# Block products by Strassen's scheme in the projections of an attention and retention block

## The chip, the cores and the metric

The kernel runs on one core of a Trainium2 chip. The metric is the device time of one execution in microseconds (us). Engines are named as in the profile: PE is TensorE (PEld its weight loads), DVE is VectorE, ACT is ScalarE, POOL is GpSimd, SP is SyncE, whose queue issues all the transfers here.

## The reference

For x of 4096 tokens by 1024 features (float32, one layer):

```python
u = rms_norm(h, pre_norm_gain)
proj = einsum('bsd,de->bse', u, w_in)                # 1024 -> 4104
fq, fk, fv, fz, ff, rq, rk, rv, rz = split(proj)     # 4 x 512, 8, 4 x 512
fox = forgetting_attention(fq, fk, fv, ff + bias)    # 8 heads of 64, causal
fox = fox * silu(fz)
ret = retention(rq, rk, rv)                          # 4 heads of 128, rotary, chunks of 64, group norm
ret = ret * silu(rz)
out = einsum('bse,ed->bsd', concat(fox, ret), w_out) # 1024 -> 1024
h = h + rms_norm(out, post_norm_gain)
```

## The kernel before, in words

Float32 precision is had from float16 matmuls: each operand is split into a high and a low float16 part, and a product is three passes, high by high, high by low and low by high (`PASSES`, line 29; `unit`, line 367). A block is 512 tokens; there are 8. A projection unit is 128 output rows by 512 columns with the whole depth of 1024, that is 8 depth steps by 3 passes: 24 matmuls of 512 columns into one PSUM bank. "T" units put output features on the partitions (queries and keys), "N" units put tokens there (values and gates). The weights come in groups of 1024 columns: group 0 and group 1 are the attention heads 0 to 3 and 4 to 7, groups 2 and 3 the retention heads, group 4 is `w_out`.

The program has three stages.

- **Group 0** (`phase_f0`, line 539). For each block: x is loaded, normalised (`a_norm`), turned by PE, split (`a_k`) and stored in DRAM as `XT`; four T units, then four N units of two matmuls each, of 256 and 264 columns because the 8 forget logits ride along. DVE and ACT evacuate.
- **Attention with fills** (`attention`, line 1035). 1152 steps of 128 keys by 512 queries. A step has on PE two score matmuls, a matmul for the running maximum of a later item (`max_tile`, DVE reduces it from PSUM) and twelve of 64 or 65 columns that apply the weights to the values; on ACT two exponentials of 512 columns; on POOL a subtraction. Between steps a generator of fills emits projection work of groups 1, 2 and 3 (`fill_f1`, `fill_r`) and the retention, as much as a credit allows: `FILL_COST` and `ATT_COST` are PE times that set the ratio, `RMIN` its floor.
- **The output projection** (`fill_o`, line 1150). It needs all heads of a block, so most of it comes after the last attention step. For each of 32 tiles of 128 tokens: row maximum and scaling, 8 transposes, a split, 48 matmuls of 512 columns, and the second norm.

Every instruction order is the program's own (`tc.manual_schedule`). Evacuations are generators (`spawn`) that go one step further at each `tick`; so each engine's queue is in the order of the ticks, and an engine whose next instruction waits holds up all behind it. PSUM is a pool of eight banks, `PS` (line 93), shared by projection units, score tiles, maxima, the attention's sums and the retention. Weights are split by `w_split` (line 210) into pools of 16 tiles a half (`wt`, `wn`), so that two groups fit; their maxima, for scaling, are taken by `scales` (line 281).

```python
    def unit(outs, lhs, rhss):
        for k in range(KT):
            for i, (pw, px) in enumerate(PASSES):
                for o, r in zip(outs, rhss):
                    mm(o, lhs(k, pw, px), r(k, pw, px), k == 0 and i == 0, k == KT - 1 and i == 2)
            yield k
```

Of the kernel before, what the change touches and what calls it, by code (L numbers as in the profile page):

```python
# [16 lines left out]
D = 1024  # L17
KT = 8
# [10 lines left out]
PASSES = ((0, 0), (0, 1), (1, 0))  # L29
COST_MM = 216.0  # L30
WARM = 28
PUMP = (2, 6)
# [7 lines left out]
FILL_COST = 1.121e6  # L40
ATT_COST = 1.05e6
# [3 lines left out]
RMIN = 1.0  # L45
FRESH = 4
# [7 lines left out]
def kernel(  # L54
# [23 lines left out]
    KC = max(8, NB + 1)  # L78
    BUFS = dict(wt=16, wn=16, rw=2, xh=8, xt=4, kc=KC, vt=KC, s4=5, xq=4, lq=2, s2=8, z1=4, pf=2, ph=6, pl=6, sm=14, mk=2, qk=4, mr=2)
# [5 lines left out]
    SHARED = {t: "b2" for t in ('s2', 'pf', 'rw')}  # L85
# [64 lines left out]
    XT = DR("XT", [NB, KT, 128, 2, 512], F16)  # L150
# [42 lines left out]
    def w_raw(g, part, k, tag="rw"):  # L193

        rows = slice(k * 128, (k + 1) * 128)
        raw = SB(tag, [128, 512 + (FH if g == 0 and part else 0)])
        if g == 4:
            dma(raw, wo2[rows, part * 512 : (part + 1) * 512])
            return raw
        base = 0 if g < 2 else 2048 + FH  # L200
        src = w2[rows, base : base + 2048].rearrange("p (s c) -> p s c", s=4)[:, 2 * part : 2 * part + 2, (g % 2) * 256 : (g % 2) * 256 + 256]
        if g == 0 and part:
            dma(raw[:, 512:520], w2[rows, 2048 : 2048 + FH])
        dma(raw[:, 0:512].rearrange("p (s c) -> p s c", s=2), src)
        return raw
# [3 lines left out]

    def w_split(g, part, k, raw, W):  # L210

        tag = w_tag(g, part)
        n = raw.shape[1]
        wt = SB(tag, [128, 2, 512 + (FH if tag == "wn" else 0)], F16)
        hi, lo = wt[:, 0, 0:n], wt[:, 1, 0:n]
        gk = gsc[g][part][:, k : k + 1]
        nc.scalar.activation(out=hi, in_=raw, func=AF.Copy, scale=gk)
        yield 1
        stt(lo, raw, gk, hi, ALU.mult, ALU.subtract)
        for _ in range(WAGE):  # L220
            yield 1
        W.append(wt)

    def w_max(mk, i, raw):
        nc.vector.tensor_reduce(out=mk[:, i : i + 1], in_=raw, axis=AX.X, op=ALU.max, apply_absolute_value=True)
# [55 lines left out]
    def scales(g):  # L281

        sets = ((0, 1),) if g == 4 else ((0,), (1,))
        for parts in sets:
            mk = SB("mk", [128, 2 * KT])
            todo = [(part, k) for part in parts for k in range(KT)]
            raws = []
            for i in range(len(todo) + 2):
                if i < len(todo):
                    raws.append(w_raw(g, *todo[i]))  # L290
                for _ in range(SAGE):
                    yield 1
                if i >= 2:
                    w_max(mk, i - 2, raws[i - 2])
# [46 lines left out]
    def a_k(b, xs, t0, k, X):  # L341
        if t0 == 0:
            X.append(SB("kc" if b % 2 == 0 else "xh", [128, 2, 512], F16))
        o = X[k]
        n = len(xs)
        until(("a", b, t0))
        p = PS()
        for t in range(n):
            nc.tensor.transpose(p[:, t * 128 : (t + 1) * 128], xs[t][:, k * 128 : (k + 1) * 128], idf)  # L349
        sl = slice(t0 * 128, (t0 + n) * 128)  # L350
        nc.scalar.copy(out=o[:, 0, sl], in_=p[:, 0 : n * 128])
        yield 1
        tt(o[:, 1, sl], p[:, 0 : n * 128], o[:, 0, sl], ALU.subtract)
        done.add(("xh", b, t0, k))
        if t0 + n == 4:
            done.add(("x", b, k))
            for _ in range(3 if b > 1 else 20 + 3 * k if b else 12 + 2 * k):
                yield 1
            dma(XT[b, k], o)

    def xt_load(b, k):
        o = SB("xh", [128, 2, 512], F16)
        dma(o, XT[b, k])
        return o


    def unit(outs, lhs, rhss):

        for k in range(KT):
            for i, (pw, px) in enumerate(PASSES):  # L370
                for o, r in zip(outs, rhss):
                    mm(o, lhs(k, pw, px), r(k, pw, px), k == 0 and i == 0, k == KT - 1 and i == 2)
            yield k

    def unit_T(W, X, col, p):
        return unit([p], lambda k, pw, px: W[k][:, pw, col : col + 128], [lambda k, pw, px: X[k][:, px, :]])

    def unit_T2(W, X, col, p, half):

        sl = slice(256 * half, 256 * half + 256)  # L380
        for k in range(KT):
            for i, (pw, px) in enumerate(PASSES):
                first, last = k == 0 and i == 0, k == KT - 1 and i == 2
                mm(p[:, sl], W[k][:, pw, col : col + 128], X[k][:, px, sl], first and not half, last and half == 1)
            yield k

    def unit_N(W, X, t, cols, ps):
        return unit(
            ps,
            lambda k, pw, px: X[k][:, px, t * 128 : (t + 1) * 128],  # L390
            [lambda k, pw, px, c=c: W[k][:, pw, c[0] : c[1]] for c in cols],
        )

    def evac_qk(p, g, b, j):
        st = SB("qk", [128, 2, 512], F16)
        f = gsc[g][0][:, KT + 2 : KT + 3]
        nc.scalar.activation(out=st[:, 0, :], in_=p, func=AF.Copy, scale=f)
# [967 lines left out]
```

## Time and profile before

| | |
|---|---|
| median of 3 runs | 3148.81 us (3147.89 to 3149.89) |
| the profiled execution: its time, its span | 3151.84 us, 3150.0 us |
| PE, PEld busy | 3029.2 us (96%), 1794.7 us (57%) |
| DVE, ACT, POOL busy | 2076.8 us (66%), 1873.1 us (59%), 1351.6 us (43%) |
| mean granted clock of TensorE | 0.985 |
| moved by DMA | 284.62 MB, 90 GB/s over the span |

A busy share is over the whole span; the stages differ. The first exponential of the attention starts at 424.8 us and the last matmul of its values ends near 2815 us, so the three stages are about 425, 2390 and 335 us long.

### The profile page before, as it was taken

To read this page: it belongs to the slowest core of one execution; us is meant where nothing else is said; L and a number is where in the kernel's file an instruction comes from. 1 tells how busy PE (TensorE), PEld (TensorE's weight loads), DVE (VectorE), ACT (ScalarE), POOL (GpSimd) and SP (SyncE) were. 2 spreads that over 40 slices of the span, in tenths; PEclk is the share of its full clock that TensorE was granted. 3 is DMA by queue.
4 is the path that set the end of the run, shared out by engine and by line. 5 is a ranking of instruction groups with operands and counts; after the bars stand their busy time and mean duration, and the time that the engine had idled before them with its cause. 6 is when DMAs were issued, how large, how long until landed. Compare 5 with 4: busy or idle time off the path is not lost.

```text
span 3150.0 us, 67744 instructions
## 1 busy us (share of the span) xinstructions
PE 3029.2 (96%) x26798; PEld 1794.7 (57%) x26799; DVE 2076.8 (66%) x4372; ACT 1873.1 (59%) x3508; POOL 1351.6 (43%) x1285
## 2 busy tenths in 40 slices
PE   8999989999999999999999999999999999889999
PEld 6666555555555555665555565556556555555554
DVE  6545567446455676777678878776877786645555
ACT  4333345676677667666667675667666766653332
POOL 0000024554555455555545564556455645540000
PEclk9999999999999999999999999999999999999999
DMA  6455753223235231311114223112111321124443
GB/s 179 156 166 152 199 123 95 67 82 93 69 88 134 64 80 35 91 51 52 55 57 101 58 71 97 51 43 78 49 51 45 111 73 33 57 68 141 141 141 120
DMA packets 266174, 284.62 MB, mean 90 GB/s; under 512 B 58976, under 2 KB 212192, under 8 KB 265856
## 3 DMA queue, kind: packets, MB, share of 16 engines
q1 hardware_dynamic: 265856, 280.30, 31.3%
q8 instruction: 210, 3.44, 0.4%
q14 instruction: 108, 0.88, 0.1%
HBM read 194.88 MB, written 88.74 MB: 90 GB/s over the span
## 4 chain that ended last, share of the span: by engine, by line
PE 80%; DVE 12%; ACT 3%; issue 2%; DMA 2%; POOL 1%; SPq 1%; POOLq 0%; DVEq 0%; ACTq 0%
PE ps L104 77%; DVE mrow L999 3%; DVE s L141 2%; DVE s L144 1%; DVE sm L141 1%; DMA rw<-in_w_in_dram 1%; ACT ph L1133 1%; PE ps L1188 1%; ACT pf L1132 1%; SPq L107 1%; PE ps L349 1%; DVE sm L144 1%; DVE s L147 1%; POOL pl L308 1%; POOL sm L308 0%
## 5 line engine op out<-in xcount | busy, mean ns | idle before, releaser
L308 POOL TENSOR_TENSOR pl<-pf,ph 128x512 f16<-128x512 f32 (+3 forms) x1152 | 1281.2, 1117 | 1135.0 <-ACT ph L1133 856.8
L1132 ACT ACTIVATE pf<-ps,gsc 128x512 f32<-128x512 f32 (+3 forms) x1152 | 758.2, 658 | 694.0 <-PE ps L104 677.0
L999 DVE TENSOR_REDUCE mrow<-ps 128x1 f32<-128x512 f32 (+3 forms) x1152 | 717.6, 641 | 356.9 <-PE ps L104 345.8
L104 PE MATMUL ps<-wn,xh 128*128 128x512 f16 (+2 forms) x3840 | 852.7, 359 | 3.1 <-DVE qk L147 2.9
L1133 ACT ACTIVATE ph<-ps,gsc 128x512 f16<-128x512 f32 (+3 forms) x1152 | 754.3, 655 | 0.0
L104 PEld LDWEIGHTS <-xh 128*128 128x128 f16 x4608 | 450.2, 98 | 450.5 <-issue 22.5
L104 PE MATMUL ps<-xh,wt 128*128 128x512 f16 x2688 | 667.7, 381 | 3.4 <-DVE mrow L999 2.0
L104 PEld LDWEIGHTS <-wt 128*128 128x128 f16 x3168 | 308.9, 98 | 356.4 <-issue 24.6
L104 PEld LDWEIGHTS <-ph 128*128 128x128 f16 x8448 | 423.9, 97 | 76.0 <-issue 8.0
L104 PE MATMUL ps<-vt,ph 128*128 128x65 f16 (+1 forms) x8448 | 433.8, 195 | 10.4 <-ACT ph L1133 7.3
L104 PE MATMUL ps<-xq,kc 99*128 99x512 f16 (+3 forms) x1152 | 420.0, 365 | 14.6 <-DMA xq<-MR 9.7
L104 PE MATMUL ps<-vt,pl 128*128 128x65 f16 x4224 | 423.4, 193 | 3.8 <-POOL pl L308 3.8
L104 PE MATMUL ps<-lq,kc 128*128 128x512 f16 (+3 forms) x1152 | 419.1, 364 | 0.0
L104 PE MATMUL ps<-kc,xq 99*128 99x512 f16 (+3 forms) x1152 | 383.1, 364 | 34.3 <-DVE mrow L999 25.1
L104 PEld LDWEIGHTS <-pl 128*128 128x128 f16 x4224 | 393.3, 99 | 5.1 <-POOL pl L308 4.7
L104 PEld LDWEIGHTS <-kc 128*128 128x128 f16 (+1 forms) x3072 | 281.9, 99 | 196.8 <-issue 22.2
L141 DVE TENSOR_TENSOR s<-s,s 64x512 f32<-64x512 f32 (+1 forms) x256 | 258.6, 1010 | 33.3 <-ACT s L755 26.3
L308 POOL TENSOR_TENSOR sm<-sm,nhalf 128x4 f32<-128x4 f32 (+2 forms) x80 | 63.0, 787 | 350.5 <-DVE sm L144 308.5
L104 PEld LDWEIGHTS <-xq 99*128 99x128 f16 x1152 | 112.3, 98 | 139.4 <-issue 9.5
L104 PE MATMUL ps<-wt,xh 128*128 128x512 f16 x768 | 184.0, 381 | 0.0
L141 DVE TENSOR_TENSOR ps<-ps,maskM 128x128 f32<-128x128 f32 x256 | 75.1, 293 | 108.4 <-PE ps L104 107.6
L141 DVE TENSOR_TENSOR xh<-ps,xh 128x256 f16<-128x256 f32 (+1 forms) x128 | 70.3, 555 | 105.5 <-ACT xh L338 86.1
(120 smaller groups left out, 2525.2 us busy)
## 6 DMA issues: line engine op xcount, KB each, us to landing
xh<-XT SPq DMA_DIRECT2D x176, 256.0 KB
rw<-in_w_in_dram SPq DMA_DIRECT2D x104, 256.0 KB
xt<-in_x_dram SPq DMA_DIRECT2D x36, 512.0 KB
s<-MX SPq DMA_DIRECT2D x32, 512.0 KB
out_dram<-xt SPq DMA_DIRECT2D x31, 512.0 KB
s<-in_x_dram SPq DMA_DIRECT2D x28, 512.0 KB
VD<-s SPq DMA_DIRECT2D x16, 516.0 KB
vt<-VD SPq DMA_DIRECT2D x64, 129.0 KB
```

The costliest lines, as they stand in the source:

```text
L104: nc.tensor.matmul(out=o, lhsT=lhsT, rhs=rhs, start=start, stop=stop, skip_group_check=True)
L107: nc.sync.dma_start(out=o, in_=i)
L141: nc.vector.tensor_tensor(out=o, in0=a, in1=b, op=op)
L144: nc.vector.tensor_scalar(out=o, in0=a, scalar1=s1, scalar2=s2, op0=op0, op1=op1)
L147: nc.vector.scalar_tensor_tensor(out=o, in0=a, scalar=s, in1=b, op0=op0, op1=op1)
L308: nc.gpsimd.tensor_tensor(out=o, in0=a, in1=b, op=op)
L349: nc.tensor.transpose(p[:, t * 128 : (t + 1) * 128], xs[t][:, k * 128 : (k + 1) * 128], idf)
L999: nc.vector.tensor_reduce(out=mrow[:, t, c : c + 1], in_=p[:, 0:w], axis=AX.X, op=ALU.max)
L1132: nc.scalar.activation(out=pf[:, q0:512], in_=st[:, q0:512], func=AF.Exp, scale=es)
L1133: nc.scalar.activation(out=ph[:, q0:512], in_=st[:, q0:512], func=AF.Exp, scale=es)
L1188: nc.tensor.transpose(p[:, e * 128 : (e + 1) * 128], mxt[:, half * 4 + e, :], idf)
```

## The change: seven products of half the depth

Depth, rows and columns of each projection are cut in two, which makes 2 by 2 blocks. Instead of the eight block products, seven are made (Strassen's scheme in Winograd's form), of sums and differences of blocks. The sums are made in float32 before the split into float16 parts, so the three passes stay. A unit is now two tiles of 128 by 256 columns side by side in a bank (one of 260 columns in the N units of group 0); a product is 4 depth steps by 3 passes by 2 tiles: 24 matmuls of 256 columns. The seven use three banks (`BANK`): bank 0 gathers products 0, 2, 4 and 5 one on top of the other, and its states after 0, 2 and 4 are copied out by ACT; DVE adds three of the four output blocks together from a bank and a copy. Products 5 and 6 are emitted after the next unit's product 0 (`flow`).

```diff
+NP = 7
+BANK = (0, 1, 0, 2, 0, 0, 2)
-FILL_COST = 1.121e6
-ATT_COST = 1.05e6
+FILL_COST = 1.012e6
+ATT_COST = 1.085e6
-RMIN = 1.0
+RMIN = 0.9
-    BUFS = dict(wt=16, wn=16, rw=2, xh=8, xt=4, kc=KC, vt=KC, s4=5, xq=4, lq=2, s2=8, z1=4, pf=2, ph=6, pl=6, sm=14, mk=2, qk=4, mr=2)
+    BUFS = dict(wt=NP, wn=NP, xh=NP, xt=4, kc=KC, vt=KC, s4=5, xq=4, lq=2, s2=12, z1=4, pf=2, ph=6, pl=6, sm=14, mk=2, qk=2, mr=2)
-    XT = DR("XT", [NB, KT, 128, 2, 512], F16)
+    XT = DR("XT", [NB, NP, 128, 4, 2, 256], F16)
+    def w_make(g, part, raws, W, pace=1, pool=True):
...
+        sub = ptt if pool else tt
...
+        yield from scale(0)
+        yield from split(0, 0, 0)
+        yield from scale(1)
+        yield from diff((0, 0), (0, 1), (0, 0))
+        yield from split(1, 1, 0)
+        yield from split(3, 0, 0)
+        yield from diff((0, 0), (1, 1), (0, 0))
+        yield from diff((0, 1), (1, 1), (0, 1))
+        yield from split(2, 0, 0)
+        yield from diff((1, 0), (1, 0), (0, 0))
+        yield from split(4, 0, 1)
+        yield from split(5, 1, 0)
+        yield from split(6, 1, 1)
+    def a_k(b, xs, k, X, first=False):
...
+        tt(c[:, 1], a11, c[:, 0], ALU.subtract)
+        tt(c[:, 0], a22, c[:, 0], ALU.add)
+        tt(d[:, 0], c[:, 0], a11, ALU.subtract)
+        tt(d[:, 1], a12, d[:, 0], ALU.subtract)
...
+        sp = [split(X, i, k, a, ptt) for i, a in ((2, d[:, 0]), (3, c[:, 0]), (4, c[:, 1]), (6, d[:, 1]))]
+    class Unit:
...
+        def prod(self, i):
+            b = BANK[i]
+            new = self.p[b] is None
+            while self.unread[b]:
+                assert chains
+                tick()
+            for k in range(4):
...
+                for n, (pw, px) in enumerate(PASSES):
+                    for t in range(self.nt):
+                        mm(
+                            p[:, t * self.w : (t + 1) * self.w],
+                            self.lhs(i, t, k, pw, px),
+                            self.rhs(i, t, k, pw, px),
+                            new and k == 0 and n == 0 and t == 0,
+                            k == 3 and n == 2,
+                        )
...
+        def post(self, i):
+            yield 1
+            if i in (0, 2, 4):
+                s = self.s[i] = SB("s2", [128, self.nt * self.w])
+                src = self.p[0][:, 0 : self.nt * self.w]
...
+            if i == 1:
+                self.add(0, 0, 1, self.s.pop(0))
...
+    def flow(units):
...
+            yield from u.prod(0)
+            if prev is not None:
+                yield from prev.prod(5)
+                yield from prev.prod(6)
+            for i in range(1, 5):
+                yield from u.prod(i)
```

At the start all the weights of one half go through `w_make` before the rest of the first block is normalised (`drain(makers[0])` in `phase_f0`). In `fill_o` two tiles make one unit; all of it now stands behind the last attention step, where about three of the 32 tiles had been ahead of it.

Where the instructions stand, at two places. DVE at the start, from the point where the weights' scale is known (`gsc`). `wt` are split weights, `xh` in the second piece raw weights, `rw` raw weights before, `xt` the second half of the first block's rows. Before:

```order
L268 RECIPROCAL gsc_8_150<-gsc_8_150 128x1
L147 SCALAR_TENSOR_TENSOR wt_367<-rw_173,gsc_8_150,wt_367 128x512
L147 SCALAR_TENSOR_TENSOR wt_370<-rw_175,gsc_8_150,wt_370 128x512
L147 SCALAR_TENSOR_TENSOR wt_373<-rw_177,gsc_8_150,wt_373 128x512
L147 SCALAR_TENSOR_TENSOR wt_397<-rw_179,gsc_8_150,wt_397 128x512
L144 TENSOR_SCALAR sm_412<-sm_376 128x2
```

Now, the last 5 of 22 such rows and what follows them:

```order
L146 TENSOR_TENSOR wt_402<-xh_174,wt_402 128x2x256
L146 TENSOR_TENSOR wt_407<-xh_175,wt_407 128x2x256
L146 TENSOR_TENSOR wt_407<-xh_176,wt_407 128x2x256
L146 TENSOR_TENSOR wt_412<-xh_175,wt_412 128x2x256
L146 TENSOR_TENSOR wt_412<-xh_176,wt_412 128x2x256
L149 TENSOR_SCALAR sm_419<-sm_363 128x2
L146 TENSOR_TENSOR sm_421<-sm_420 128x2
L146 TENSOR_TENSOR sm_421<-sm_421,sm_419 128x2
L149 TENSOR_SCALAR sm_421<-sm_421 128x2
L152 SCALAR_TENSOR_TENSOR sm_420<-sm_420,sm_421 128x2
L149 TENSOR_SCALAR xt_185<-xt_185,sm_420 128x1024
L149 TENSOR_SCALAR xt_187<-xt_187,sm_420 128x1024
```

The norm of the second half of the block (`sm`, `xt`) came between the fourth and the fifth weight split; now it comes behind all 22 instructions on the weights, and on PE the 32 transposes that need it stand ahead of the first product.

DVE in the attention, where a retention block's keys are rotated. `mrow` are the maxima that free a PSUM bank each, `s` (`qk`) the keys and the rotation table. Before:

```order
L999 TENSOR_REDUCE mrow_24734<-ps_24836 128x1
L147 SCALAR_TENSOR_TENSOR sm_24843<-mr_24841,ps_24839 4x128
L144 TENSOR_SCALAR mr_24841<-sm_24843 4x128
L141 TENSOR_TENSOR s_4853_24846<-s_4843_24819,s_4749_24363 64x512
L999 TENSOR_REDUCE mrow_24734<-ps_24868 128x1
L999 TENSOR_REDUCE mrow_24734<-ps_24871 128x1
L141 TENSOR_TENSOR s_4853_24846<-s_4843_24819,s_4749_24363 64x512
L141 TENSOR_TENSOR s_4843_24819<-s_4843_24819,s_4749_24363 128x512
```

Now:

```order
L152 SCALAR_TENSOR_TENSOR s_4690_26470<-ps_26213,gsc_12_154,s_4630_26211 128x256
L152 SCALAR_TENSOR_TENSOR s_4691_26471<-ps_26213,gsc_12_154,s_4630_26211 128x256
L146 TENSOR_TENSOR s_4757_26872<-s_4690_26470,s_4548_25747 64x512
L146 TENSOR_TENSOR s_4758_26874<-s_4691_26471,s_4548_25747 64x512
L146 TENSOR_TENSOR s_4757_26872<-s_4690_26470,s_4548_25747 64x512
L146 TENSOR_TENSOR s_4758_26874<-s_4691_26471,s_4548_25747 64x512
L146 TENSOR_TENSOR s_4690_26470<-s_4690_26470,s_4548_25747 128x512
L146 TENSOR_TENSOR s_4691_26471<-s_4691_26471,s_4548_25747 128x512
L146 TENSOR_TENSOR s_4690_26470<-s_4690_26470,s_4757_26872 128x512
L146 TENSOR_TENSOR s_4691_26471<-s_4691_26471,s_4758_26874 128x512
L152 SCALAR_TENSOR_TENSOR s_4771_26937<-ps_26876,gsc_13_155,s_4713_26611 128x512
```

Sums out of PSUM (the rows that read `ps`) are new on DVE, and the rotations of two heads stand in one row of eight, where one head's four stood among the maxima.

## Rows read from the trace of the kernel before

**Rows 1.** The page: busy us, share and instructions of each engine.

```profile
PE 3029.2 (96%) x26798; PEld 1794.7 (57%) x26799; DVE 2076.8 (66%) x4372; ACT 1873.1 (59%) x3508; POOL 1351.6 (43%) x1285
```

**Rows 2.** Stretches: length, then busy us (instructions) of PE, PEld, DVE, ACT, POOL, PEclk, DMA.

```profile
62.00:425.00 363.00, 350.84 (x2457) 243.43 (x2456) 190.10 (x569) 129.77 (x299) 10.10 (x20) 0.99 0.57 168
425.00:1180.00 755.00, 741.96 (x7015) 411.01 (x7013) 443.40 (x883) 501.97 (x915) 398.08 (x376) 0.99 0.35 88
1180.00:2815.00 1635.00, 1556.60 (x15357) 939.67 (x15356) 1212.80 (x2379) 1107.34 (x2038) 917.88 (x821) 0.98 0.22 63
2475.00:2550.00 75.00, 69.47 (x657) 42.34 (x656) 65.05 (x136) 55.69 (x107) 38.78 (x36) 1.00 0.44 135
...
2815.00:3150.00 335.00, 327.66 (x1641) 163.89 (x1637) 190.80 (x441) 106.53 (x204) 22.11 (x60) 0.99 0.42 133
```

**Rows 3.** Timeline of PE where nothing waits: start us, us, instruction, count.

```profile
150.86 1.49 PE L104 MATMUL ps<-wn,kc 128*128 128x256 f16 x12
152.19 0.38 PE L349 MATMUL ps<-csb,s 128*128 128x128 f32 x2
...
3127.38 0.60 PE L1188 MATMUL ps<-csb,s 128*128 128x128 f32 x4
3127.82 2.11 PE L104 MATMUL ps<-wt,xh 128*128 128x512 f16 x9
...
3132.14 5.34 PE L104 MATMUL ps<-wn,xh 128*128 128x512 f16 x24
3137.32 5.34 PE L104 MATMUL ps<-wt,xh 128*128 128x512 f16 x24
```

**Rows 4.** Timeline at the start, and the attention's first exponential.

```profile
22.27 1.95 ACT L217 ACTIVATE wt<-rw,gsc 128x512 f16<-128x512 f32 x3 [9.37 <-DVE gsc L144]
23.04 0.61 PE L104 MATMUL ps<-kc,wt 128*128 128x256 f16 x2 [1.28 <-ACT wt L217]
23.29 2.06 DVE L147 SCALAR_TENSOR_TENSOR wt<-rw,gsc,wt 128x512 f16<-128x512 f32 x3
...
424.84 0.69 ACT L1132 ACTIVATE pf<-ps,gsc 128x512 f32<-128x512 f32 x1
```

**Rows 5.** The chain that ended last, in order of time: two T parts of group 0.

```profile
123.03 23.20 PE ps L104 x128
...
169.60 23.20 PE ps L104 x128
```

**Rows 6.** Groups of DVE by shape: count, busy us, mean ns, idle before.

```profile
L141 DVE TENSOR_TENSOR s<-s,s 128x512 f32<-128x512 f32 x128 | 136.7, 1068 | 2.3
L225 DVE TENSOR_REDUCE mk<-rw 128x1 f32<-128x512 f32 x72 | 48.4, 673 | 13.1 <-DMA rw<-in_w_in_dram 13.1
L147 DVE SCALAR_TENSOR_TENSOR qk<-ps,gsc,qk 128x512 f16<-128x512 f32 x64 | 47.3, 743 | 35.9 <-ACT qk L397 35.6
L141 DVE TENSOR_TENSOR xh<-ps,xh 128x512 f16<-128x512 f32 x64 | 44.3, 692 | 86.1 <-ACT xh L338 86.1
L1177 DVE TENSOR_REDUCE sm<-s 128x1 f32<-128x1024 f32 x32 | 38.6, 1208 | 0.0
L147 DVE SCALAR_TENSOR_TENSOR s<-z,s 128x256 f32<-128x256 f32 x64 | 33.6, 524 | 6.8 <-ACT z L853 6.7
L147 DVE SCALAR_TENSOR_TENSOR wn<-rw,gsc,wn 128x512 f16<-128x512 f32 x32 | 30.2, 945 | 16.3 <-ACT wn L217 16.2
...
L141 DVE TENSOR_TENSOR xh<-ps,xh 128x256 f16<-128x256 f32 x64 | 26.0, 419 | 19.4 <-ACT xh L351 19.1
```

**Rows 7.** Groups of ACT and of POOL by shape: the costliest of each.

```profile
L1132 ACT ACTIVATE pf<-ps,gsc 128x512 f32<-128x512 f32 x960 | 665.5, 693 | 556.6 <-PE ps L104 543.4 <-issue 2.4 <-POOL pl L308 2.1
...
L308 POOL TENSOR_TENSOR pl<-pf,ph 128x512 f16<-128x512 f32 x960 | 1149.4, 1201 | 965.5 <-ACT ph L1133 713.8 <-PE ps L104 194.6 <-issue 28.3
```

**Rows 8.** Waits of PE: us in total, times, longest us.

```profile
PE ps L104 <- DVE mrow L999: 34.5, 37, 4.2
```

**Rows 9.** Timeline of the end: the last matmuls' evacuation.

```profile
3142.70 0.60 ACT L1197 ACTIVATE s<-ps 128x512 bf16<-128x512 f32 x1 [4.43 <-PE ps L104]
```

More of the change, by code (lines that the diff above doesn't have):

```diff
@@ L207, in w_tag @@
     def w_tag(g, part):
         return ("wt", "wn")[part if g < 4 else 1 - part]
-    def w_split(g, part, k, raw, W):
+    wfree = {"wt": NP, "wn": NP}
+    def w_make(g, part, raws, W, pace=1, pool=True):
+        w = w_cols(g, part)
         tag = w_tag(g, part)
-        n = raw.shape[1]
[L214 to L222, printed above, removed]
@@ L224, in w_max, with seg, each, split @@
-    def w_max(mk, i, raw):
-        nc.vector.tensor_reduce(out=mk[:, i : i + 1], in_=raw, axis=AX.X, op=ALU.max, apply_absolute_value=True)
+        half = len(raws) // 2
+        sub = ptt if pool else tt
+        def seg(j, c):
+            return raws[j][1][:, :, c, :]
+        def each(rows):
+            return range(rows * half, (rows + 1) * half)
+        def split(i, rows, c):
+            while not wfree[tag]:
+                yield 1
+            wfree[tag] -= 1
+            o = SB(tag, [128, 4, 2, w], F16)
+            n = 4 // half
+            for j in each(rows):
+                nc.scalar.copy(out=o[:, (j % half) * n : (j % half) * n + n, 0, :], in_=seg(j, c))
+            for _ in range(pace):
+                yield 1
+            for j in each(rows):
+                sl = slice((j % half) * n, (j % half) * n + n)
+                tt(o[:, sl, 1, :], seg(j, c), o[:, sl, 0, :], ALU.subtract)
+            W[i] = o
+            for _ in range(pace):
+                yield 1
@@ new lines, in scale, with diff @@
+        def scale(rows):
+            for j in each(rows):
+                k, r = raws[j]
+                for i in range(r.shape[1]):
+                    rr = r[:, i].rearrange("p s c -> p (s c)")
+                    nc.scalar.activation(out=rr, in_=rr, func=AF.Copy, scale=gsc[g][part][:, k + i : k + i + 1])
+                for _ in range(pace):
+                    yield 1
+        def diff(o, a, b):
+            for j in range(half):
+                sub(seg(o[0] * half + j, o[1]), seg(a[0] * half + j, a[1]), seg(b[0] * half + j, b[1]), ALU.subtract)
+            for _ in range(2 * pace):
+                yield 1
@@ L378, in unit_T2 @@
[L378 to L392, printed above, removed]
@@ new lines, in units @@
+        def units():
+            for n in range(0, NT, 2):
+                while n not in Xs:
+                    advance()
+                    if n not in Xs:
+                        yield None
+                yield unit_O(n)
+        while not ready(0) or ("loaded", 4) not in done or not all(("gn", h, NB - 1) in done for h in range(RH)):
+            yield WAIT + pump(PUMP)
+        fetch(1)
+        start = gstep[0] + OAGE
+        while attn_alive[0] and gstep[0] < start:
+            yield -1
@@ L1252, in fill_o @@
+        for k in flow(units()):
+            yield WAIT if k is None else 3 * COST_MM + pump(k)
+            if k == 1:
+                c = advance()
+                if c:
+                    yield c
         flush()
```

951 lines of the change are left out of this document (582 added, 369 removed).

## The prediction

> **What bounds the kernel now.** I read the page's busy shares first, then the stretches, then PE's timeline where nothing waits, then the waits. PE is busy for 96% of the span [rows 1]. A busy PE need not be a full one, so the reader should look at its rate: in the output projection 24 matmuls of 512 columns take 3137.32 - 3132.14 = 5.18 us, 0.2158 us each, with nothing between them [rows 3]. That is the full clock and no gap. By stretches [rows 2], PE idles 12.2 of 363 us in group 0, 13.0 of 755 in the part of the attention that has group 1 as its fill, 78.4 of 1635 in the part with retention fills, and 7.3 of 335 at the end. So PE bounds all three stages, and what takes work from PE can shorten each. The second thing to see in the same rows is where PE's idle time grows: 1.7% where DVE is busy 59% (443 of 755), 4.8% where it is busy 74% (1213 of 1635), 7.4% where it is busy 87% (65.05 of 75). PE's largest wait on another engine is for DVE's maxima: 34.5 us in 37 waits [rows 8]. DVE is not the bound, but the fuller its queue, the more often PE waits for a bank.
>
> **What it takes from PE.** One matmul of 256 or 264 columns, each behind its own weight load, is in the trace: 12 take 152.19 - 150.86 = 1.33 us, 0.1108 us at 260 columns on average, so 0.1091 at 256 [rows 3]. Halving the columns per weight load costs 1% (two of 0.1091 for one of 0.2158). Before, the projections are 6912 matmuls of 512 columns and 768 pairs of 256 and 264: 1491.6 + 170.2 = 1662 us. Now PE's order has 12096 of 256 columns and 1344 of 260: 1319.7 + 148.9 = 1469 us. 193 us go: 40 in group 0 (336 to 295.5), 144 in the attention (4743 x 0.2158 = 1023.5 to 8064 x 0.1091 = 879.8), 9 at the end. There the whole output projection now stands, where before 1401 of 1536 matmuls stood: 302 us become 293. Transposes keep their number but for 16 more at the start, 0.11 us each (4 in 0.44 us [rows 3]).
>
> The weight loads are where a rule speaks against the change. The row shows them hidden: PEld is busy for less time than PE in every stretch [rows 2], and the 12 matmuls above leave no gap. The Trainium skill (TensorE: Matmul & The Clock Gate, Back-to-back issue gap) says that in a stream of weight loads and matmuls both set the spacing, about 81 ns at 128 columns where the matmul alone gives 56. As an estimate from that page, 25 ns more on each of 13440 matmuls would add 336 us. The sum goes by the row, which was taken at this very width.
>
> **What it adds elsewhere, and the group 0 stage.** At the start the first product now stands behind all 22 DVE instructions on the first half's weights. From 22.3 us, six ACT operations of 0.65 us, 22 of DVE at 0.69 (2.06 for three), some 3.5 us of changes between the two, 3.5 for the norm of the second half-block and 32 transposes of 0.11 put the first product at about 52 us, not at 23.04 [rows 4]. The block itself is 168 x 0.1091 + 168 x 0.1108 = 36.9 us of products and 3.5 of transposes, and its second half waits for 14 more weight splits and four maxima of 1.2 us on a DVE that is behind; I put 9 us there. Block 0 then ends near 102 us. Before, block 1's T part begins one period of 46.57 us ahead of that of block 2 [rows 5], which puts the end of block 0 near 80 us. So 22 us are lost. The period then falls from 46.6 to 41.3 us (36.9 + 3.5 + 0.9 for the running sums), 289 us for seven blocks. Before, the seven took 345 (80 to 425), 19 over their period; I keep these 19. DVE's work in the stage, its 867 instructions at the prices of rows 6, comes to about 345 us where the stretch had 190 of 363 and the start some 35: it would be over 80% busy, and I add 10 us. Group 0 ends at 102 + 289 + 19 + 10 = **420 us**, 5 earlier. Bounds: 390 if DVE keeps up and the start waits less, 450 if DVE sets the pace.
>
> **The attention.** PE's busy time falls by 144 and by 3 for transposes that move to the end: 38 of it in the group 1 part (742 to 704 us), 109 in the rest (1557 to 1448). On DVE, by [rows 6] or the nearest shape: it loses 48 maxima of weights (0.673), 48 weight splits (0.945), 32 low parts of queries and keys (0.743), 64 evacuations of 256 columns (0.419), 64 gates (0.524) and 10 us of the output projection: 172 us. It gains 84 weight splits (0.945), 24 maxima (1.208), 96 sums of 512 columns from a bank (0.692 to 0.743), 96 of 256 (0.419), 24 low parts from SBUF (1.068, the row of a tensor_tensor with two such inputs) and 8 at 0.743, 64 smaller evacuations (32) and 32 gates of 512 (34): 316. Net 143, of which 57 in the group 1 part: 500 us there and 1299 in the rest. ACT gains 40 us net: 120 copies of a bank's state (0.69) and 84 casts of weights replace narrower evacuations; with 1609 + 40 us it stays near 72%, under the cover of PE. POOL gets 48 differences of weights at 1.2 us [rows 7], 58 us on 1316. If that cover went, their price would be bounded by these sums.
>
> With DVE at 500 of 730 us (69%) the line through [rows 2] gives PE 3.8% idle; at 1299 of 1550 (84%), 6.8%. So 704 / 0.962 = 732 and 1448 / 0.932 = 1554. After the last fill product 36 of the 1152 score steps follow with nothing beside them: ACT's two exponentials (1.39 us [rows 7]) then set the step and not PE's 1.0, 13 us. The attention takes **2299 us**, against 2390: 91 less, of 144 that leave PE. Bounds: 2230 and 2470 (rivals).
>
> What else moves: loads of x go from 176 of 256 KB to 154 of 512 KB, 46 to 81 MB, and stores from 17 to 29. Each load has at least six products (16 us of PE's own time) between the release of its tile and its use, and the DMA engines are busy 0.22 to 0.35 there [rows 2]; I cost it at nothing, up to 30 us if SP's queue holds one behind another wait. The weight pools now hold one group, not two, so a group's splits begin only as the last unit lets its tiles go. A unit's seven products (18 us alone, some 40 among score steps) cover 14 splits and the differences (some 25 us): nothing, up to 25 us at each of three changes.
>
> **The end.** 293.5 us of products and 256 transposes x 0.109 = 28 us. The first pair's preparation, four operations of 1.2 us, then transposes and copies, no longer overlaps with attention: 12. After the last product 7.3 us as before [rows 9], and 9 for waits, since DVE goes from 57% to about 80% there. **350 us**, 15 more; bounds 335 and 375.
>
> **Sum.** 420 + 2299 + 350 = 3069 us of span, 81 under the 3150.0 of the profiled execution. That one took 3151.84 us, 3.0 above the median of the runs; against the median of 3148.81 the forecast is **3068 us**, 2.6% faster.
>
> **Rivals.**
> - *Faster still.* DVE's longer queue may cost PE nothing, since the sums it does now are not what frees score tiles. Then idle shares stay at 1.7% and 4.8%: 716 + 1521 + 13 = 2250, group 0 400, the end 340: 2990 us. For it: in the part with group 1 and at the end PE idles little. Against: the three stretches of [rows 2] rise in order.
> - *Slower: banks.* A unit held one bank for 24 matmuls; now bank 0 stays from product 0 to product 5 of its unit, over nine products, bank 2 over five, bank 1 over one. Per unit of seven products that is 15 / 7 = 2.1 banks on average instead of 1 of the eight, and at the same time PE comes back to each bank sooner. Each wait for a maximum costs 34.5 / 37 = 0.93 us [rows 8]. PE's need in the attention is 2152 us and its idle time was 91; with 13 for the last steps, about 130 more waits, one in 18 of the 2304 maxima and score tiles, use up the gain of the whole change. With one in ten, 230 x 0.93 = 214 us: 2470, with group 0 at 430 and the end at 360: 3260 us. Against it: PE waited for maxima 37 times in 1152 so far.
> - *No change.* The start and DVE give all back: group 0 450 us, the end 370, the attention 2328: 3148 us.
> - *Weight loads.* They are not hidden after all when they come twice as often for long: by the page 3068 + 336 = 3404 us. From rows: PEld's share of PE in [rows 2] is 0.55 to 0.7 before and would be at most 1.0, so that a gap could open only where both are full.
>
> **How the numbers follow.** My forecast has a chance of 0.50 (3010 to 3120), the faster rival 0.25, the banks 0.15, no change 0.07, the weight loads 0.03. A measurement of this kernel tells apart about 0.2%, 6 us. Faster: 0.50 + 0.25 and a little of the third, 0.76; same 0.06; slower 0.15 + 0.03, 0.18. The range of 2955 to 3200 leaves out the weight loads, the upper part of the banks (0.10) and the far end of the faster rival (0.05).
>
> **What would show it.** Products: 24 matmuls of 256 columns in 2.62 us wherever nothing waits. Start: first product near 52 us, block 0's end near 102. The first exponential near 420, the last attention matmul near 2720. DVE busy about 84% and PE idle about 7% in the retention part, with the maxima still PE's first cause. The forecast is wrong in its mechanism if PE's waits on score or maximum banks exceed 200 us, if ACT's state copies appear as PE's largest wait, or if 24 products take over 2.7 us in a stretch without waits.

## The result, and the profile after

The changed kernel takes **3470.02 us** (median; 3468.61 to 3471.8) against 3149.35 of the kernel before on the same chips: a ratio of 1.1016, 95% interval 1.0997 to 1.1035. It is 10% slower, where 2.6% faster was forecast, and the time lies outside the stated range of 2955 to 3200. The profiled execution has a span of 3470.0 us.

Its stretches, with the first 62 us (the attention runs from the first exponential to the last matmul on the values; columns as in [rows 2]):

```profile
0.00:62.00 62.00, 29.25 (x156) 18.31 (x157) 43.80 (x97) 31.23 (x68) 12.97 (x24) 0.76 0.68 211
62.00:557.00 495.00, 354.92 (x2959) 298.65 (x2958) 307.13 (x762) 223.07 (x538) 150.47 (x181) 0.89 0.47 141
557.00:1330.00 773.00, 732.62 (x8549) 557.71 (x8547) 511.04 (x954) 547.99 (x996) 436.03 (x403) 0.98 0.36 104
1330.00:3074.00 1744.00, 1525.93 (x17111) 1150.82 (x17109) 1260.16 (x2439) 1098.67 (x1974) 951.14 (x837) 0.94 0.22 68
3074.00:3470.00 396.00, 340.90 (x2945) 298.82 (x2944) 243.42 (x536) 174.58 (x337) 156.18 (x176) 0.94 0.40 129
sum 3470.00, PE 2983.62 PEld 2324.31 DVE 2365.56 ACT 2075.55 POOL 1706.80; mean PE 596.72 PEld 464.86 DVE 473.11 ACT 415.11 POOL 341.36
```

Every stage is longer: group 0 takes 557 us (425 before), the attention 2517 (2390), the end 396 (335). PE idles 486 us in all (3470.0 - 2983.6), where it idled 121. The granted clock fell with it, from 0.985 to 0.937 over the span, that is, the lower of its two levels being half, from some 95 us spent there (2 x 0.015 x 3150) to some 440 (2 x 0.063 x 3470). PE's busy time fell by only 46 us, not by 193. The clock accounts for most of what is missing: PE was busy for 293 us at the lower level, where it had been for 72, and by the ratio of the levels that is an estimated 110 us more.

The products themselves do what they should. In PE's timeline 24 matmuls of 256 columns start at 78.80 and the next product at 81.42, 2.62 us later, as forecast:

```profile
78.80 2.78 PE L109 MATMUL ps<-ph,wt 128*128 128x256 f16 x24
81.42 0.83 PE L109 MATMUL ps<-wn,kc 128*128 128x260 f16 x6
```

**Group 0.** What PE waits for between 62 and 557 us (us, times, longest):

```profile
PE ps L109 <- ACT s L557: 86.7, 8, 18.1
PE ps L109 <- ACT s L555: 34.0, 22, 8.3
```

These are the copies of bank 0's states. One such wait, on each of the three queues that have a part in it. SP, ACT, PE:

```profile
108.48 4.13 SPq L112 DMA_DIRECT2D XT<-xh  x5
112.67 1.11 SPq L112 DMA_DIRECT2D KX<-in_aux_dram  x1
113.84 4.42 SPq L112 DMA_DIRECT2D QX<-in_aux_dram  x1
118.31 3.04 SPq L112 DMA_DIRECT2D s<-in_x_dram  x4
...
127.43 1.06 ACT L400 ACTIVATE s<-s 128x1024 bf16<-128x1024 f32 x1 [13.22 <-DMA s<-in_x_dram]
...
138.27 0.68 ACT L557 ACTIVATE s<-ps,gsc 128x512 f32<-128x512 f32 x1
...
139.00 4.18 PE L109 MATMUL ps<-xh,wt 128*128 128x256 f16 x24 [15.04 <-ACT s L557]
```

The copy itself takes 0.68 us. It stands in ACT's queue behind the squares of the next block's norm (L400), and these wait for rows of x that SP issued only at 118.31, behind the stores of the split rows and the constants. PE stands meanwhile, because the product that is next in its order adds to the same bank. The pattern comes six times, with waits of 15.0, 11.6, 13.3, 12.0, 13.0 and 18.1 us. Nor is PE at its full rate at once. Three stretches around the wait show the granted clock (the third number from the end):

```profile
123.90:139.00 15.10, 0.07 (x1) 0.00 (x0) 5.71 (x20) 6.61 (x13) 1.96 (x3) 0.64 0.65 217
139.00:143.00 4.00, 4.00 (x24) 3.05 (x24) 3.69 (x13) 0.00 (x0) 0.70 (x2) 0.64 0.02 4
143.00:160.00 17.00, 14.54 (x131) 12.56 (x130) 13.63 (x32) 9.99 (x27) 6.86 (x10) 1.00 0.19 40
```

The clock fell while PE stood (1.00 up to 128 us, 0.50 from 130 to 141, 1.00 again from 142), and the 24 matmuls behind the wait take 4.0 us instead of 2.62.

**The attention.** PE's waits from 557 to 3074 us, where [rows 8] had 34.5 us in 37 waits:

```profile
PE ps L109 <- DVE mrow L1284: 123.2, 101, 6.6
PE ps L109 <- DVE s L152: 39.4, 19, 4.8
PE ps L109 <- POOL pl L380: 31.7, 30, 5.8
PE ps L109 <- ACT ph L1418: 17.1, 23, 4.3
```

The second line shows the sums out of banks that the change added. PE idles 258 us here, where it idled 91. Of the 167 us more, the waits for maxima hold 89, those for DVE's other results, the sums above all, 43, and those for POOL's subtractions 28 (4 before, 32 now). A typical wait for a maximum, from the timelines of DVE, POOL and PE:

```profile
1516.89 0.68 DVE L146 TENSOR_TENSOR s<-qk,s 64x512 f32<-64x512 f32 x1
1517.60 5.13 DVE L146 TENSOR_TENSOR qk<-qk,s 128x512 f32<-128x512 f32 x4
...
1517.77 4.41 POOL L380 TENSOR_TENSOR pl<-pf,ph 128x512 f16<-128x512 f32 x3 [1.35 <-ACT ph L1418]
...
1522.65 0.28 DVE L146 TENSOR_TENSOR ps<-ps,maskM 128x128 f32<-128x128 f32 x1
1522.97 0.29 DVE L1284 TENSOR_REDUCE mrow<-ps 128x1 f32<-128x128 f32 x1
...
1523.31 0.32 PE L109 MATMUL ps<-kc,xq 99*128 99x384 f16 x1 [3.77 <-DVE mrow L1284]
```

The last four operations of two heads' rotations stand in one row on DVE, 1.28 us each. The maximum that frees a bank, and the mask that it needs, stand behind them.

**The end.** From the last exponential to the first product:

```profile
3085.60 3.68 PE L1485 MATMUL ps<-csb,s 128*128 128x128 f32 x16 [11.55 <-ACT s L1464]
3089.10 0.40 PE L109 MATMUL ps<-wn,xh 128*128 128x256 f16 x1
```

and PE's waits from 3074 us on:

```profile
PE ps L109 <- ACT s L555: 24.4, 15, 2.8
PE ps L1485 <- ACT s L1464: 11.6, 1, 11.6
PE ps L109 <- DVE xh L146: 8.8, 11, 3.5
```

So of the 55 us that PE idles there, 24 are state copies, 12 the preparation of the first pair and 9 waits for split rows (`xh`).

### The profile page after: what moved, and what is told of

Read it like the earlier page. It is cut to its first block, busy times and chain, and to the rows that moved or that the text cites. A ratio compares the mean times of both kernels' runs of the same rounds, so it can differ in the third digit from the quotient of the medians.

```text
span 3470.0 us, 78970 instructions
## 1 busy us (share of the span) xinstructions
PE 2983.6 (86%) x31711; PEld 2324.3 (67%) x31711; DVE 2365.6 (68%) x4785; ACT 2075.5 (60%) x3912; POOL 1706.8 (49%) x1621
## 5 line engine op out<-in xcount | busy, mean ns | idle before, releaser
L109 PE MATMUL ps<-wn,xh 128*128 128x256 f16 (+1 forms) x5856 | 890.1, 279 | 55.5 <-ACT s L555 39.7
L109 PEld LDWEIGHTS <-xh 128*128 128x128 f16 x7008 | 697.6, 100 | 301.1 <-issue 118.2
L109 PEld LDWEIGHTS <-wt 128*128 128x128 f16 x5376 | 540.6, 101 | 315.6 <-issue 164.4
L109 PE MATMUL ps<-xh,wt 128*128 128x256 f16 x4704 | 627.6, 281 | 44.4 <-ACT s L557 42.8
L109 PEld LDWEIGHTS <-ph 128*128 128x128 f16 x8544 | 449.4, 99 | 33.4 <-issue 11.9
L109 PE MATMUL ps<-vt,ph 128*128 128x65 f16 (+1 forms) x8448 | 452.1, 197 | 4.5 <-DVE mrow L1284 3.7
L109 PEld LDWEIGHTS <-kc 128*128 128x128 f16 (+1 forms) x2688 | 246.7, 100 | 134.1 <-issue 68.8
L109 PE MATMUL ps<-wt,xh 128*128 128x256 f16 x1152 | 267.1, 279 | 0.0
L146 DVE TENSOR_TENSOR s<-ps,s 128x512 f32<-128x512 f32 (+2 forms) x280 | 154.0, 550 | 113.0 <-ACT xh L1489 46.0
L380 POOL TENSOR_TENSOR xh<-s,xh 128x256 f16<-128x256 f32 (+1 forms) x112 | 97.7, 901 | 92.4 <-ACT xh L1489 63.7
```

The lines of the kernel that those rows point to most:

```text
L109: nc.tensor.matmul(out=o, lhsT=lhsT, rhs=rhs, start=start, stop=stop, skip_group_check=True)
L146: nc.vector.tensor_tensor(out=o, in0=a, in1=b, op=op)
L380: nc.gpsimd.tensor_tensor(out=o, in0=a, in1=b, op=op)
```

## The experiments

Where no interval is given, a time is that of a single run, beside the kernel before on the same chip (3144.8 to 3151.6 us). The rows of stretches below are the attention alone, and PE's idle time is length less PE's busy time. A stage that an edit leaves alone repeats within a few us (of the kernels with early loads, group 0 takes 473 to 476 us), but the attention differs by up to 10 us between kernels whose edit lies in group 0 alone (2517, 2511 and 2506 us).

**Group 0: whose wait is it?** Two edits, one of when ACT and DVE get the next block's norm, one of SP's order alone.

The late norms:

```diff
-                if n == 4:
+                if n == 14:
                     spawn(a_norm(xa[0:2], ("a", b, 0)))
-                if n == 14:
+                if n == 20:
                     spawn(a_norm(xa[2:4], ("a", b, 2)))
```

> Only the ticks at which ACT and DVE get the next block's norm in group 0 are moved: the first half from tick 4 to tick 14 of a block, the second from 14 to 20. Theory: in six blocks ACT stands at the norm's square, whose rows of x have not landed, and the copy of bank 0's state stands behind it in ACT's queue; PE then waits 12 to 18 us a block, 83 us in all, and runs at the lower clock for some microseconds after. Then PE's waits for the state copies of T units (87.6 us) fall below 15 us, the first exponential of the attention comes near 460 us instead of 557, and the span near 3375. Rival: the state copy itself, or the bank that the next product shares with it, is what is late; then the waits stay above 60 us and the span within 20 us of 3470.

The early loads:

```diff
-                    xa = a_load(b + 1, 0, 4, "s4" if b else "xt")
+                    xa = ahead.pop() if ahead else a_load(b + 1, 0, 4, "xt")
...
+                if n == at[-1] + 6 and b + 1 < NB:
+                    ahead.append(a_load(b + 1, 0, 4, "s4"))
                 if n == at[-1] + 8:
                     spawn(x_store(b, nxt[0][0]))
```

> The norm stays at tick 4, but the rows of x of the block after next are issued two ticks ahead of the stores of the split rows, not behind them. Theory as in the run with the late norm: the rows then land before the norm, ACT does not stand, the waits for state copies of T units fall below 20 us and the first exponential comes near 455 us; if the loads only move the wait (SP stands for a free tile, and the stores and the query and key transfers behind it), the gain is less than half of that. Rival (the copy or the bank itself is late): no change of more than 20 us.

Late norms: 3433.5 us, 36 less. Only half of the wait for T units' copies went (87 to 44.5 us, not below 15): ACT's squares still wait 55 us for rows of x, where they waited 74, so that ten and six ticks more are not enough for loads that come that late. Early loads: **3379.0 us**, 91 less, with the first exponential at 474.6 us, about 20 later than expected. PE's waits in group 0 are then

```profile
PE ps L109 <- ACT s L555: 27.4, 20, 6.7
PE ps L109 <- DVE sm L152: 16.2, 6, 5.9
PE ps L109 <- ACT s L557: 11.7, 9, 3.1
```

The copies of T units cost 11.7 us instead of 86.7. This is shown, then: 83 of the 137 us by which group 0 missed its forecast are SP's order, by way of ACT's. No run takes the other 54 apart. The attention changes by no more than the 10 us named above:

```profile
474.60:2981.00 2506.40, 2244.47 (x25652) 1700.75 (x25650) 1771.30 (x3392) 1643.79 (x2970) 1386.01 (x1240) 0.96 0.27 79
```

The kernels below marked "early" have this edit, and this row is what they are compared with.

**The attention: DVE's order.** The second head's rotations start later.

```diff
-                spawn(rope_turn(..., ("rope", ret.g, ret.b, 2 * col + t)))
+                spawn(rope_turn(..., ("rope", ret.g, ret.b, 2 * col + t), 6 * t))
...
-    def rope_turn(o, rp, key):
-        yield 1
+    def rope_turn(o, rp, key, late):
+        for _ in range(1 + late):
+            yield 1
```

> The rotations of the second head of a pair start 6 ticks later, so that eight of them no longer stand in one row on DVE. Same work. Theory: maxima stand in DVE's queue behind rows of vector work (rotations, splits, norms); the part of PE's idle time of the attention that leads back to rotations of keys and queries (about 32 us of 254) then falls below 15 us, and with the clock's share the attention (2517 us) is 30 to 60 us shorter. Rival: PE lacks banks, whatever DVE's order; then the attention changes by less than 15 us.

3458.0 us; the attention takes 2505 us, 12 less, which is hardly more than the 10 us by which kernels with the same attention differ. The waits for maxima fell from 123 to 108 us, those for DVE's sums rose from 39 to 46, and PE idles as long as before (256 us). The order of the rotations alone is at most a small part. By the expectation this is what want of banks would give, but the runs below show that DVE's work has a price too.

**The attention: banks.** One bank less (`bufs=7`) in the kernel before and in the changed one (early), and two less (`bufs=6`) in the kernel before:

```diff
-        return psp.tile([128, 512], F32, tag="ps", ..., bufs=8)
+        return psp.tile([128, 512], F32, tag="ps", ..., bufs=7)
```

> The kernel before with seven PSUM banks instead of eight, which takes about as much from the attention as the change does with its units of 2.1 banks instead of 1. Rival (banks): the attention is 100 us or more longer than 2390, with PE's waits for maxima and score banks over 120 us. Theory (DVE's queue): a bank less is worth 10 to 40 us, and the span stays below 3200.

> The kernel before with six PSUM banks. The first bank taken away cost 38 us of the span (attention 2390 to 2422). Theory A (banks): the cost of a bank rises steeply as they get few; span 3290 or more, attention 2500 or more as in the changed kernel, with PE idle near 200 us there and many more stretches at the lower clock. Theory B: about as much again, span 3210 to 3250.

> The changed kernel with early loads (its attention took 2506 us, PE idle 262) with seven PSUM banks instead of eight. Theory A (banks): with 2.1 banks held by units on average, PE already has little room to run ahead of the engines that empty banks, so one more bank gone costs far more than the 32 us that it cost the kernel before: attention 2600 us or more. Theory B (DVE's queue alone): about the same 32 us as before, attention 2520 to 2550.

The kernel before takes 3188.2 us with seven banks and 3257.1 with six, its attention 2422 and 2487 us (2391 with eight). With eight banks and with six:

```profile
424.80:2815.40 2390.60, 2299.17 (x22379) 1351.18 (x22377) 1656.24 (x3261) 1609.51 (x2955) 1315.96 (x1196) 0.99 0.26 71
433.60:2920.50 2486.90, 2330.01 (x22377) 1351.79 (x22376) 1654.27 (x3261) 1615.55 (x2954) 1315.70 (x1196) 0.98 0.25 68
```

The changed kernel (early) takes 3488.2 us with seven; its attention goes from 2506 to 2616:

```profile
474.20:3089.80 2615.60, 2273.80 (x25654) 1701.42 (x25654) 1778.18 (x3393) 1650.42 (x2970) 1380.59 (x1240) 0.95 0.26 76
```

A bank costs the kernel before 31 us, a second one 65, the changed kernel 109. That its units hold 2.1 banks and not 1 would bring it to where banks are dear; this fits the numbers, but no run that shortens the hold alone shows it. And two banks less did not make the kernel before look like the changed one: its clock stays at 0.98 and PE idles 157 us, not 258. Its span of 3257 us lies between the two expectations, close to the lower one.

**Fewer banks held.** The fills (early) emit a unit's seven products in a row.

```diff
+            if not ahead:
+                for i in range(NP):
+                    yield from u.prod(i)
+                continue
             yield from u.prod(0)
...
-        for k in flow(fill_units()):
+        for k in flow(fill_units(), False):
```

> The changed kernel with early loads; the fills emit products 0 to 6 of a unit one after the other, without the next unit's product 0 ahead of products 5 and 6. Banks held by a unit fall from 15/7 = 2.1 to 11/7 = 1.6 on average, but product 5 comes right behind product 4, whose state ACT has to copy first. Theory A (banks): PE's waits for maxima and score banks fall by a third, and the attention gets 30 us or more shorter in spite of some waits for the state copy. Theory B (DVE's queue): no gain; the 48 copies cost 1 to 2 us each where nothing lies between, and the attention is 0 to 60 us longer.

3373.8 us, the attention 2501: no gain worth the name. Its waits show why:

```profile
PE ps L109 <- DVE mrow L1291: 86.1, 66, 6.0
PE ps L109 <- ACT s L557: 60.5, 39, 2.8
```

The waits for maxima fell by a third (122 us with early loads alone), and the state copies, now with nothing between product 4 and product 5, took it back. So the hold of banks is not priced by this run. With one bank that gathers four products the choice is between these two.

**DVE's work.** Left out of the changed kernel (early), and added to the kernel before.

In `rope_turn` of the changed kernel:

```diff
-        tt(t2[0:64], o[64:128], rp[64:128, 1, :], ALU.mult)
...
-        tt(o, o, t2, ALU.add)
```

In `rope_evac` of the kernel before, for both half products:

```diff
-        tt(t2[0:64], o[64:128], rp[64:128, 1, :], ALU.mult)
+        for _ in range(3):
+            tt(t2[0:64], o[64:128], rp[64:128, 1, :], ALU.mult)
```

> The changed kernel with early loads, without the rotary rotations of the retention's queries and keys (256 DVE instructions, about 240 us of DVE's 1240 in the retention part; they are left out of the computation). Theory B (DVE's queue): PE's idle time in the attention falls by more than its share, from 262 to 150 or less, and the attention from 2506 to 2380 or less, with the clock. Theory A (banks): maxima are emptied as late as before, since a bank is missing and not time on DVE; less than 50 us.

> The kernel before with more work for DVE: each of the two half products of a rotation is made three times, 256 more DVE instructions of about 0.94 us, the same sum (some 240 us) that the changed kernel got back 126 us of its attention for when it was left out. If DVE's work has that price at any time (DVE as such sets the pace), the attention is 100 us or more longer than 2390. If it is dear only where banks are few (DVE late and banks short together), it costs 20 to 70 us here, where units hold one bank.

Without rotations the changed kernel takes 3252.6 us, its attention 2380 (126 less for 231 us of DVE's busy time, 1771.3 to 1540.0). PE's idle time falls from 262 to 178 us, not to the 150 expected:

```profile
475.60:2855.90 2380.30, 2202.43 (x25649) 1680.37 (x25649) 1540.00 (x3136) 1641.56 (x2970) 1349.13 (x1240) 0.97 0.29 83
```

The kernel before with more of them takes **3393.0 us**; the whole loss is in its attention (group 0 takes 424 us and the end 335, as before):

```profile
424.20:3056.50 2632.30, 2387.63 (x22378) 1385.10 (x22377) 1908.01 (x3517) 1611.22 (x2954) 1347.15 (x1196) 0.95 0.23 64
```

DVE is busy 252 us longer than before (1656 to 1908) and the attention is 242 us longer. That is almost one for one, with eight banks and one bank a unit. In its totals it looks like the changed kernel: PE idles 245 us, the clock is at 0.95. My guess of 20 to 70 us, had want of banks been needed for it, fell here. But PE's waits are not shared out alike:

```profile
PE ps L104 <- DVE mrow L1001: 88.3, 68, 4.2
PE ps L813 <- DVE s L141: 56.2, 14, 5.8
```

The second line are the retention's transposes, which need the rotated keys themselves. The longer rotations stand on that path too, and the changed kernel waits there for only 4 us. So 0.96 us for each us of DVE's work is an upper value for the changed kernel, and 0.55, taken in it, the nearer one.

**Both together.** The changed kernel (early), without rotations and with seven banks.

> The changed kernel with early loads, without the rotations (left out of the computation) and with seven PSUM banks. With the rotations a bank cost 110 us of the attention (2506 to 2616); without them and with eight banks it took 2380. If lateness of DVE and want of banks multiply, a bank costs 30 to 70 us here: 2410 to 2450. If each has its own price, 110 again: 2490.

3354.3 us, the attention 2480: a bank costs 100 us without the rotations, 109 with them. So each has a price of its own; they hardly multiply.

**PE's time by itself.** An eighth of the products taken out of the kernel before.

```diff
             for i, (pw, px) in enumerate(PASSES):
+                if i == 2 and 4 <= k < 7:
+                    continue
```

> The kernel before with 21 of the 24 matmuls of each unit: the third pass (low weights by high x) is left out at depth steps 4 to 6. TensorE loses an eighth of its products, about what the seven products take away (some 205 us: 40 in group 0, 127 in the attention, 38 at the end), and nothing else changes: no sums, no state copies, one bank a unit. If TensorE's work is worth its full time everywhere, the span falls by 190 to 210, to about 2950. If DVE sets the pace of the retention part already, as the run with more work for DVE suggests, the attention gives back at most half of its 127 us, and the span is 3010 or more.

3005.1 us, 140 less than the run beside it; the stages are 397, 2309 and 297 us.

```profile
397.10:2706.50 2309.40, 2183.75 (x21787) 1295.83 (x21784) 1658.43 (x3261) 1600.53 (x2954) 1318.17 (x1196) 0.98 0.26 73
```

At the end all 38 us came back, in group 0 28 of 40, in the attention 81 of 127: PE is busy 115 us less there and idles 34 us more, most of them in waits for DVE. My "at most half" was too low, 190 to 210 for the span too high. (The stages are compared with the execution of 3150.0 us, the time with the run beside it.) This is about what seven products could bring if they cost nothing elsewhere: 4.4%.

**Attempts to mend it** (all three early). Rotations spread, with one `yield` more between the four operations, and those of the second head on GpSimd:

```diff
-                spawn(rope_turn(...))
+                spawn(rope_turn(..., t, ptt if t else tt))
...
```

Products 0 and 1 of the first unit ahead of the other weights, with the rest of the first block and the loads and norm of the second moved to later ticks, and a lower pace of the fills; the third kernel has all of it together:

```diff
-FILL_COST = 1.012e6
+FILL_COST = 0.99e6
-RMIN = 0.9
+RMIN = 0.8
...
-        drain(makers[0])
+        while 1 not in W[0]:
+            next(maker)
+        chains.append(maker)
...
```

> The changed kernel with early loads; the rotations of a pair's two heads are spread (one every other tick, the heads in turn) and those of the second head go to GpSimd, some 120 us of DVE's work. Where GpSimd runs, a DVE operation with two SBUF inputs takes up to 1.3 us in the trace instead of 0.68, so that part of the relief may be given back. Theory (DVE's rows of vector work against too few banks): without any rotation the attention was 126 us shorter; with half of the work gone from DVE and the rows broken up, 40 to 80 us shorter than 2506. If POOL's subtractions come late instead (PE waits for them 32 us so far), the gain is under 20 us and those waits exceed 80 us.

> The changed kernel with early loads and two more edits in places apart. At the start the first T unit's products 0 and 1 no longer stand behind the 22 DVE instructions on the weights and the second half's norm: first product near 30 us instead of 45, first exponential near 460 instead of 475 if the weights of the other products keep up, unchanged if the second half's weights (whose scale came at 58 us) set the start. In the attention the fill's pace is set 2% lower, so that the last 36 score steps have products beside them: attention 10 to 20 us shorter than 2506, and some retention work moves behind it, 0 to 10 us.

> Early loads, spread rotations with half on GpSimd, early first products and the lower pace together, with the chip timed against the kernel before. If the gains add up, 3260 to 3320; still slower than 3149, since the waits that are left in the attention (maxima and score banks, about 150 us), the end (396 us against 335) and the lower clock are not touched.

With rotations on GpSimd: 3394.4 us, the attention 2521, 15 longer. DVE's load fell by only 63 us (to 1708), POOL's rose by 169 (1386 to 1555), since a 128 x 512 operation of a rotation takes 1.57 us there, and the waits changed hands:

```profile
PE ps L109 <- POOL pl L380: 99.7, 64, 4.8
PE ps L109 <- DVE mrow L1290: 90.4, 93, 5.4
```

Early start and lower pace: 3364.3 us. The first product starts at 22.65 us instead of 44.75, but the first exponential at 474.1 as without it: behind the first two products PE waits again, for splits on ACT and POOL and for rows normed on DVE, and block 1's T part starts at 108.92 us (108.72 with early loads alone). The attention is 2462 us, 45 shorter (10 to 20 expected), and the end 426, 30 longer (0 to 10 expected), since retention work moved there. All together: 3373.3 us, ratio 1.0698 (1.068 to 1.0716), not 3260 to 3320 and no better than the early start and pace alone. No version beats the kernel before.

## Why the prediction was wrong

The three stages missed by 137, 218 and 46 us, together the 401 from 3069 to 3470.

- **Group 0, "the period then falls from 46.6 to 41.3 us"; "I keep these 19"; "10 us".** The start came out near its forecast (block 1's T part at 110.65 us, 102 forecast), in part by luck: the first product came 7 us early (44.75, 52 forecast), and block 0 then took 66 us, not 50. The period was not near. It is 62.9 us ((488.14 - 110.65) / 6 between T parts). I summed PE's work and DVE's load and left out the order in the two queues between them: the new stores of split rows stand ahead of the x loads on SP, the norm that needs them stands ahead of the state copy on ACT. That ACT stays "under the cover of PE", as I put it for the attention, holds only while nothing ahead of its copies waits. The forecast did name SP's queue as a risk, but for the attention's loads alone, and at nothing to 30 us. With early loads the first exponential comes at 475; this fault alone is 83 us, and the period 48.4 us then ((302.21 - 108.72) / 4); the waits that are left are small and many.
- **The attention, "the line through [rows 2]".** DVE's load was forecast well: 500 + 1299 us, measured 511 + 1260. So was PE's price for a product at full clock. What failed is the step from load to time. I read PE's idle share off DVE's busy share (6.8% at 84%). Measured are 12.5% idle (1744 - 1526 of 1744) at a DVE share of 72%. A busy share is no measure of how late an engine that works in order is, and DVE's work costs from half to nearly the whole of its own length here: 126 us for 231 removed (e5), 242 for 252 added (e11).
- **"38 and 109 us" for PE's time.** What is taken from PE in the attention comes back to two thirds (81 of 127, e13). The line, with nothing added to DVE, would give back some 130 of the 147, over four fifths.
- **The banks.** That a missing bank costs time is real, but the rival's price was set by "0.93 us" for each wait. Measured: 31 us of attention for the first bank less, 65 for the second, 109 for one less in the changed kernel.
- **A budget.** An estimate from the runs, as if their prices added up: the seven products -81; DVE's 115 us more (1656 to 1771) at 0.55 to 0.96 each +63 to +110; 1.1 banks more at 31 to 109 each +34 to +120. That makes +16 to +149 us; measured are +126 (2391 to 2517). The split between the last two is not settled closer than this. POOL's 71 us more (1316 to 1387), most of it differences of weights, is left out: PE's waits for POOL's subtractions grew by 28 us and stayed when the rotations went (31 us in e5), and no run tests what they cost.
- **The clock.** No term of the forecast had it. PE's work was priced at the clock of the kernel before, but a stall costs more than its length. The 218 us of the attention are 111 of more idle time (258 against 147 with the last steps) and 107 of longer busy time (2259 against 2152). PE was busy there for 214 us at the lower level, for 51 before; that is an estimated 82 of the 107.
- **The end.** PE's work came out as forecast (busy 341 of 396 us, 321.5 forecast at full clock), and the clock (0.94) goes with the 19 us that it is busy longer. "9 for waits" was 24 for state copies and 9 for split rows, though DVE was busy 61% and not about 80%. The first pair cost 12 as forecast.
- **The other rivals.** Weight loads are hidden at this width, 2.62 us for 24 matmuls of 256 columns, though PEld's share of PE rose to 0.75 to 0.88 in the four stages (0.50 to 0.69 before, not from 0.55). The 25 ns of the Trainium skill (TensorE: Matmul & The Clock Gate, Back-to-back issue gap), given for 128 columns, do not show at 256. "Faster still", that DVE's longer queue costs PE nothing, is the opposite of what e5 and e11 showed. The slower case had a chance of 0.18, and its time of 3260 left out group 0's wait and the clock. Of the three signs named for a wrong mechanism one came: state copies are PE's largest wait (87.6 + 58.5 = 146 us over the whole span, 125 for maxima). Waits for maxima (125 us) and for the exponentials that free score banks (at most 20) stayed under the 200, and 24 matmuls without waits under 2.7 us.

## What to carry to other kernels

An algorithm that saves time on the engine with the highest busy share pays only where no other engine, in order and with bursts, is as near to its limit: add dummy work to the second engine, or take work from the first without adding any, and the price of each is known in two runs. Before a forecast, walk through each in-order queue around a new short instruction and ask what stands ahead of it and what that waits for; a 0.7 us copy here cost waits of 12 to 18 us. Count accumulator banks held over time as a resource like any engine, and price one by taking it away.

## What the hardware showed

- A DVE operation on two SBUF operands slows beside POOL. In the rows of 1516 to 1522 us above one of 64 x 512 takes 0.68 us while POOL stands, and the four of 128 x 512 that follow, beside three subtractions on POOL, 1.28 us each (over the whole trace such operations take 0.68 too where POOL stands); POOL's take 1.47 instead of 1.16. The maxima, which read PSUM, keep their 0.68 us. The Trainium skill (SBUF — State Buffer, Who interferes with whom) says that DVE with two SBUF inputs and GpSimd reading SBUF share one port pair, held for a whole instruction. The trace agrees that the two slow each other. It does not show that one waits out the other's whole instruction: one after the other the four and the three would take 6.2 us, and they took 5.13. It fits that rotations on GpSimd gained nothing, but no run shows how much of that is the shared ports.
- The granted clock falls to its lower level in a wait and stays there for some microseconds of work behind it (0.50 from 130 to 141 us around the end of one wait at 139, 1.00 from 142 on). Stalls of 12 to 18 us cost 1.4 to 2.2 us each on top: the next 24 matmuls show 4.13 to 5.01 us in the timeline, where 2.78 stands at the full clock.
- Eight banks or seven is no detail: 31 us in one kernel, 100 to 109 in the other, for the same edit.
